# Two-layer hybrid decoder trunk: maxima spread by DRAM transfers, recurrence by pairs, one norm ahead of its transposes, six late value chunks

## Chip, cores and metric

The kernel runs on one core of a Trainium2 chip. The metric is the device time of one execution in microseconds, as the median of the runs. A profile is one execution of its own, with its own time.

## What is computed

256 tokens of width 1024 go through two layers. Layer 0 mixes tokens with an mLSTM of 4 heads, layer 1 with an RG-LRU recurrence of width 768; both add cross-attention over 256 memory tokens. Each mixer is followed by an output projection and a norm, and each of these by PEER (128 x 128 experts, chosen by the top 16 of two key halves) and a second norm. Cut to what the change touches:

```python
# mLSTM, here as one block of 256 tokens instead of chunks
F  = cumsum(log_sigmoid(f))              # 4 heads x 256 tokens
M  = running_max(i - F)                  # the gate maxima
w[s, t] = exp((i - F)[s] - M[t])  for s <= t, else 0
h  = (w * (k q)) v / max(|den|, exp(-(F + M)))
# RG-LRU
r, g = sigmoid(x W_a + b_a), sigmoid(x W_x + b_x)
a  = exp(-8 r softplus(-lam));  u = sqrt(1 - a*a) * g * x
h[t] = a[t] * h[t-1] + u[t];    y = h * gelu(gate)
# after each mixer and each PEER
x  = (x - mean) * rsqrt(var + eps) * g + b
```

## The kernel before, in words

All large products run on TensorE as three float32r passes: every operand is split into a high part (a rounded copy, wH) and a low part (wL = w - wH), and `mm3` (L161) forms H·H + H·L + L·H. Small products (`fp32`, L221) run in full fp32, which the trace shows as two matmuls each. The weights come from DRAM as a single list of chunks of 128 x up to 1024 (`plan`, L1080). SP loads them into five raw buffers (`load`, L116), ScalarE casts wH (L96), VectorE or GpSimd subtracts wL (`pump`, L76; `pool_cols` says how many columns GpSimd takes). A ring of three holds the split chunks (`hl`), and `EXTRA` = 3 more (`eH`, `eL`) stand in the mixer's memory for its output projection. `next` (L132) takes the next chunk, splits up to three ahead, and calls `tick` (L147), which advances one step of each generator given to `beside`. So side work enters the engines' queues one step per chunk. Every engine runs its queue in the written order.

**Layer 0** (`mlstm_layer`, L470). The keys and gates are projected first (7 tiles of `w0kg`). Beside the query projection (8 chunks of `w0qx`, `proj_t`) runs `gates` (L510): log sigmoid, the scans F and M, and `keys` (L547), which copies the keys, scaled, out of PSUM on VectorE. Then the memory projection `mem_kv` (L379, 4 chunks). After it M, which stands in 4 partitions, is spread to all 128: `sel` holds a row of ones per head, and for each head TensorE forms sel·M and adds the causal mask by an identity product (L575 to 578), and ScalarE takes the exponential with a bias per partition (L580, L581). Then come the products of keys and queries, multiplied with these weights on VectorE (L589), the cross-attention scores, and the value projection.

**Layer 1** (`rglru_layer`, L663). After the projections and a convolution, `xattn_scores` queues the softmax; three chunks of the output projection are split ahead into `eH`, `eL`, cast and subtracted on VectorE (L715 to 717). Then for six column tiles the gate products and sigmoids (L720 to 732), then `lru` (L733): decay for all six tiles, `xattn_out` (transposes, copies by ScalarE and VectorE in turn, products, split), one square root over all six tiles (L744), and then, for each pair of tiles, the scan, the gate and the split (L754 to 760). The output projection (`proj_n`, L178) runs its chunks in the order 6, 7, 0, 1, 2, 3, 4, 5; with `tail` = 6 the last six chunks are kept: their products for the first 128 tokens all come first, those for the second half last, and the norm of the first half runs beside the latter (`early`).

**Norm** (`norm`, L250) is a generator, whose steps are called between products. `add` adds the bank to x and `half` takes statistics, `stats` the variance, `center` and `spread` scale on VectorE, `scale_beside` on ScalarE and GpSimd, `turn` transposes into xH and xL. **PEER** (`peer_layer`, L916) runs 128 chunks of u, in whose second half the chosen weights are scattered, then 128 chunks of v (`products`, L1044); the last three are kept (`late`) so that the first half's norm can begin. Layer 0's last norm scales, transposes the first two of eight column tiles, scales the rest and leaves the other transposes to steps beside the next projection; ahead of it stands the memory projection of layer 1 with chunks already split. Layer 1's last norm stores the output in quarters.

## Time and profile before

| | us |
|---|---|
| median of 3 runs (1865.24 to 1870.0) | 1867.91 |
| profiled execution: its own time | 1865.7 |
| its span | 1863.9 |
| TensorE busy | 1821.8 (98%) |
| VectorE busy | 1298.0 (70%) |
| ScalarE busy | 940.3 (50%) |
| GpSimd busy | 428.7 (23%) |
| moved from and to DRAM | 333 MB, 179 GB/s |

Times inside the execution count from the start of the span. A TensorE row shows 128 x 128 weights and the columns that pass; rows of the order of time merge neighbouring instructions of one line (xN) and name in brackets the idle time of the engine before them and what ended it. PE is TensorE, DVE VectorE, ACT ScalarE, POOL GpSimd, SP the queue that issues most transfers.

### The profile page before, as it was taken

Reading aid. Unit: us, or ns where it says so; the run is one execution under the profiler, and the core shown is the slowest. Engines: PE = TensorE matmul, PEld = TensorE weight load, DVE = VectorE, ACT = ScalarE, POOL = GpSimd, SP = SyncE. Lnnn points to the kernel's source line nnn. Section 1 sums busy time; section 2 is a strip of 40 time slices with the busy share of each in tenths; the row PEclk is TensorE's granted clock in tenths of the full one; section 3 lists DMA queues with packets and bytes.
Section 4 is the critical chain, followed back from the end, with each engine's and each line's share of the span. In section 5 each row is a group of like instructions: output and inputs, shape, how many; then the busy total and the mean of one; then the engine's idle time right before and its main releaser. Section 6 shows DMA issues by size and latency. Waiting matters only on the chain.

```text
span 1863.9 us, 33272 instructions
## 1 busy us (share of the span) xinstructions
PE 1821.8 (98%) x12770; PEld 1675.5 (90%) x12770; DVE 1298.0 (70%) x2665; ACT 940.3 (50%) x1604; POOL 428.7 (23%) x326
## 2 busy tenths in 40 slices
PE   8999999999999999999998899999999999999997
PEld 8898999999999888888887699999999988888886
DVE  6474579689998555666556638695999975555556
ACT  5454555455545444555537255554555454555543
POOL 2005772343331000000010258425333300000001
PEclk9999999999999999999999899999999999999999
DMA  7465556655555666667644166666555566666664
GB/s 244 132 178 171 179 177 191 199 174 161 165 163 162 196 195 193 193 215 227 205 169 139 59 193 177 198 192 192 160 161 165 162 179 193 193 193 194 193 194 132
DMA packets 94344, 333.42 MB, mean 179 GB/s; under 512 B 10600, under 2 KB 12904, under 8 KB 93928
## 3 DMA queue, kind: packets, MB, share of 16 engines
q1 hardware_dynamic: 93320, 328.66, 58.3%
q10 hardware_dynamic: 864, 2.62, 0.4%
q8 instruction: 100, 1.64, 0.4%
q14 instruction: 60, 0.49, 0.1%
HBM read 330.19 MB, written 1.05 MB: 178 GB/s over the span
## 4 chain that ended last, share of the span: by engine, by line
PE 72%; issue 15%; POOL 7%; DVE 3%; ACT 1%; DMA 1%; SPq 0%; POOLq 0%; ACTq 0%; DVEq 0%
PE bank L164 23%; PE bank L165 23%; PE bank L163 23%; POOL wL L106 7%; PE bank L222 3%; DVE wL L111 1%; DMA raw<-in_w0kg_dram 1%; ACT wH L96 0%; DMA raw<-in_w0qx_dram 0%; DVE xc L700 0%; PE bank L314 0%; DVE aa L747 0%; DVE x L293 0%; POOL wL L109 0%; DVE x L288 0%
## 5 line engine op out<-in xcount | busy, mean ns | idle before, releaser
L96 ACT CAST wH<-raw 128x1024 fp32r<-128x1024 f32 (+2 forms) x608 | 632.3, 1041 | 791.0 <-PE bank L165 330.2
L111 DVE TENSOR_TENSOR wL<-raw,wH 128x1024 fp32r<-128x1024 f32 (+3 forms) x413 | 468.5, 1137 | 455.7 <-ACT wH L96 455.1
L163 PE MATMUL bank<-xHL,wH 128*128 128x256 f32 x2536 | 717.6, 283 | 5.9 <-ACT wH L96 4.5
L165 PE MATMUL bank<-xHL,wL 128*128 128x256 f32 x2536 | 704.5, 278 | 7.3 <-DVE wL L111 7.3
L164 PE MATMUL bank<-xHL,wH 128*128 128x256 f32 x2536 | 704.5, 278 | 0.2
L165 PEld LDWEIGHTS bank<-xHL,wL 128*128 128x128 f32 x2536 | 479.1, 189 | 9.3 <-DVE wL L111 9.1
L163 PEld LDWEIGHTS bank<-xHL,wH 128*128 128x128 f32 x2536 | 479.1, 189 | 6.6 <-ACT wH L96 4.5
L164 PEld LDWEIGHTS bank<-xHL,wH 128*128 128x128 f32 x2536 | 479.6, 189 | 0.9 <-DVE xHL L219 0.9
L165 PE MATMUL bank<-wH,cL 128*128 128x512 f32 x1024 | 398.4, 389 | 0.0
L164 PE MATMUL bank<-wL,cH 128*128 128x512 f32 x1024 | 398.3, 389 | 0.0
L163 PE MATMUL bank<-wH,cH 128*128 128x512 f32 x1024 | 398.3, 389 | 0.0
L109 POOL TENSOR_TENSOR wL<-raw,wH 128x1024 fp32r<-128x1024 f32 (+1 forms) x121 | 258.1, 2136 | 211.7 <-ACT wH L96 181.1
L165 PEld LDWEIGHTS bank<-wH,cL 128*128 128x128 f32 x1024 | 192.2, 188 | 40.0
L163 PEld LDWEIGHTS bank<-wH,cH 128*128 128x128 f32 x1024 | 192.2, 188 | 39.9
L164 PEld LDWEIGHTS bank<-wL,cH 128*128 128x128 f32 x1024 | 192.2, 188 | 39.8
L106 POOL TENSOR_TENSOR wL<-raw,wH 128x386 fp32r<-128x386 f32 x126 | 129.7, 1029 | 279.9 <-DVE wL L104 279.9
L303 POOL TENSOR_TENSOR x<-x,raw 128x256 f32<-128x256 f32 x7 | 5.3, 760 | 614.4 <-ACT x L300 614.4
L878 DVE TENSOR_TENSOR oh<-iota,i12T 128x1024 f16<-128x1024 f16 x128 | 130.5, 1020 | 0.0
L104 DVE TENSOR_TENSOR wL<-raw,wH 128x640 fp32r<-128x640 f32 x126 | 104.0, 825 | 7.4
L881 DVE TENSOR_TENSOR oh<-oh,gT 128x1024 f16<-128x1024 f16 x128 | 90.1, 704 | 4.4
L1011 PE MATMUL bank<-oh 128*128 128x128 f16 x1024 | 81.1, 220 | 1.1 <-DVE oh L881 1.1
L1011 PEld LDWEIGHTS <-oh 128*128 128x128 f16 x1024 | 58.9, 98 | 6.0 <-DVE oh L881 1.5
(269 smaller groups left out, 1524.1 us busy)
## 6 DMA issues: line engine op xcount, KB each, us to landing
raw<-in_u_dram SPq DMA_DIRECT2D x256, 512.0 KB, 3.7
raw<-in_v_dram SPq DMA_DIRECT2D x256, 512.0 KB, 4.3
raw<-in_w_q_dram SPq DMA_DIRECT2D x32, 512.0 KB, 3.7
raw<-in_w_out_dram SPq DMA_DIRECT2D x16, 512.0 KB, 4.5
raw<-in_w0qx_dram SPq DMA_DIRECT2D x8, 512.0 KB, 4.7
raw<-in_wkv_dram SPq DMA_DIRECT2D x8, 512.0 KB, 4.7
raw<-in_w1x_dram SPq DMA_DIRECT2D x8, 512.0 KB, 4.4
raw<-in_w0v_dram SPq DMA_DIRECT2D x8, 384.0 KB, 3.7
```

The source lines that it names most:

```text
L96: (nc.vector.tensor_copy if self.cast_dve else nc.scalar.copy)(h[:, c], r[:, c])
L104: nc.vector.tensor_sub(l[:, k:], r[:, k:], h[:, k:].bitcast(F32))
L106: nc.gpsimd.tensor_sub(l[:, :k], r[:, :k], h[:, :k].bitcast(F32))
L109: nc.gpsimd.tensor_sub(l[:, :k], r[:, :k], h[:, :k].bitcast(F32))
L111: nc.vector.tensor_sub(l[:, k:], r[:, k:], h[:, k:].bitcast(F32))
L163: mm(out, sH, mH, start=start, stop=False, skip_group_check=True)
L164: mm(out, sH, mL, start=False, stop=False, skip_group_check=True)
L165: mm(out, sL, mH, start=False, stop=stop, skip_group_check=True)
L222: self.nc.tensor.matmul(out, lhsT, rhs, start=start, stop=stop, skip_group_check=True)
L878: nc.vector.tensor_tensor(flat(oh[:, 1:3]), self.iota2.unsqueeze(1).to_broadcast([P, 4, P, 2]), pairs(self.i12T[:, j]), op=ALU.is_equal)
L881: nc.vector.tensor_tensor(flat(oh[:, 0:2]), two.rearrange("p z (q e t) -> p z q e t", q=2, t=2), pairs(self.gT[:, j]), op=ALU.mult)
L1011: nc.tensor.matmul(wp[:, qs], oh[:, 2, q // 2, :, q % 2], oh[:, z, q // 2, :, q % 2], start=z == 0, stop=z == 1, skip_group_check=True)
```

## The change

Layer 0: `sel` and its products go. M is stored to a DRAM tile of 4 x 256 and loaded back twice, each time to all 128 partitions, into `pw`, both on ScalarE's queue, from two new last steps of `gates`; GpSimd adds the mask to the diagonal blocks. The gates are cut into more steps, the keys are scaled by ScalarE, and the last step runs in `mem_kv`. Layer 1: decay, root, scan and gating go by pairs of tiles, the first pair's decay after the second of the six gate products; the transposes of the cross-attention come before the sixth; copies and mixer splits go to VectorE; four chunks instead of three are split ahead, with wL by GpSimd, as for the rest of the output projection, which keeps four chunks instead of six. Layer 0's second norm (`fill`) scales everything, splits two more chunks, and does all transposes before the last memory chunk. Layer 1's PEER keeps six value chunks, three of them in buffers `ends` where the low half of the weights lay, and its norm takes the second half's last 512 columns in two steps and stores in another order. The diff, cut to its core:

```diff
 def proj_n(self, splits, stat, order=range(DT), tail=0, hook=(-1, None)):
-        own, ring = late[:EXTRA], late[EXTRA:]
+        own, ring = late[:tail - HL_BUFS], late[tail - HL_BUFS:]
-    def split_to(self, dH, dL, src):
-        self.nc.scalar.copy(dH, src)
+    def split_to(self, dH, dL, src, cast=None):
+        (cast or self.nc.scalar.copy)(dH, src)
 def norm(self, y, last, early, fill=False):
+        fine = early or last
+        if last:
+            root(0)
+            nc.vector.tensor_scalar(nm, mv[:, 0, 0:1], rs[:, 0:1], -1.0, op0=ALU.mult, op1=ALU.mult)
+            scale_beside(0, 2)
+            scale(0, 2, 2), store(nc.sync, 0, 2, 2)
+            store(nc.sync, 0, 0, 2)
+            yield
+            half(*add(1, 0))
+            yield
+            half(*add(1, 1))
+            yield
+            half(*add(1, 2)), stats(1)
+            center(1, 0, 2), root(1)
+            spread(1, 0, 2), store(nc.scalar, 1, 0, 2)
+            center(1, 2, 2)
+            for q in (2, 3):
+                spread(1, q, 1), store(nc.sync, 1, q, 1)
+            return
...
+        if fill:
+            center(1, 0, 2), root(1), spread(1, 0, 2)
+            scale(0, 2, 2), scale(1, 2, 2)
+            self.release("g", "b")
+            self.pump(self.n_got + 2 + HL_BUFS)
+            yield
+            for q in (0, 2):
+                for tt in range(2):
+                    turn(tt, q, 2)
             return
 def mem_kv(self, chunks=None, hook=None):
         for c in range(4):
+            if hook and c == 3:
+                hook()
 def mlstm_layer(self):
-            sel = w.tile([4, 4, P], F32, name="sel")
+            row = ctx.enter_context(tc.tile_pool(name="row", bufs=1, space=DRAM)).tile([4, T], F32, name="row")
+            pw = w.tile([P, 4, 384], F32, name="pw")
...
                 nc.vector.tensor_scalar(M, M, -1.0, None, op0=ALU.mult)
+                yield
+                nc.scalar.dma_start(row, M)
...
                 nc.vector.tensor_scalar(c8, l6, -8.0, None, op0=ALU.mult)
+                yield
+                every = lambda n, o: bass.AP(tensor=row.tensor, offset=row.offset + o, ap=[[0, P], [T, 4], [1, n]])
+                nc.scalar.dma_start(pw[:, :, 0:T], every(T, 0))
+                nc.scalar.dma_start(pw[:, :, T:384], every(P, P))
+                diag = bass.AP(tensor=pw.tensor, offset=pw.offset, ap=[pw.ap[0], [384, 4], [T, 2], [1, P]])
+                nc.gpsimd.tensor_tensor(diag, diag, maskn.unsqueeze(1).unsqueeze(1).to_broadcast([P, 4, 2, P]),
+                                        op=ALU.add)
             def keys(t0, t1):
-                        nc.vector.tensor_scalar(kT[rows, h, part, :], src[rows], 192.0 ** -0.5, None, op0=ALU.mult)
+                        nc.scalar.activation(kT[rows, h, part, :], src[rows], AF.Copy, scale=192.0 ** -0.5)
             qx = self.proj_t(8, X)
-            self.finish_sides()
...
             self.mem_kv()()
+            self.finish_sides()
...
             for h in range(4):
-                W = self.bank()
-                self.fp32(W[:, 0:T], sel[:, h, :], M, True, False)
-                self.fp32(W[:, 0:P], self.ident, maskn, False, True)
-                self.fp32(W[:, T:384], sel[:, h, :], M[:, P:T], False, False)
-                self.fp32(W[:, T:384], self.ident, maskn, False, True)
-                nc.scalar.activation(pw[:, h, 0:T], W[:, 0:T], AF.Exp, bias=ac[:, 0, h:h + 1])
-                nc.scalar.activation(pw[:, h, T:384], W[:, T:384], AF.Exp, bias=ac[:, 1, h:h + 1])
+                nc.scalar.activation(pw[:, h, 0:T], pw[:, h, 0:T], AF.Exp, bias=ac[:, 0, h:h + 1])
+                nc.scalar.activation(pw[:, h, T:384], pw[:, h, T:384], AF.Exp, bias=ac[:, 1, h:h + 1])
 def rglru_layer(self):
-            self.pump(self.n_got + 2 + EXTRA)
+            self.pump(self.n_got + 2)
+            self.pool_cols = D
+            self.pump(self.n_got + 3 + EXTRA)
+            self.pool_cols = MIX_COLS
+            def decay(b):
+                for i in (2 * b, 2 * b + 1):
+                    nc.gpsimd.tensor_mul(rr[:, 1, i, :], xc[:, i, :], rr[:, 1, i, :])
+                    nc.scalar.activation(aa[:, i, :], rr[:, 0, i, :], AF.Exp, scale=c8[:, i:i + 1])
+                    nc.scalar.activation(th[:, i, :], rr[:, 0, i, :], AF.Tanh, scale=n8[:, i:i + 1])
+                    nc.vector.tensor_mul(rr[:, 0, i, :], aa[:, i, :], aa[:, i, :])
+                    nc.vector.scalar_tensor_tensor(th[:, i, :], rr[:, 0, i, :], 1.0, th[:, i, :],
+                                                   op0=ALU.add, op1=ALU.mult)
+            def root(b):
+                nc.scalar.activation(fl(th, b), fl(th, b), AF.Sqrt, bias=self.tiny)
+            def scan(b):
+                nc.vector.tensor_mul(fl(th, b), fl(th, b), fl(rr[:, 1], b))
+                for i in (2 * b, 2 * b + 1):
+                    nc.vector.tensor_tensor_scan(aa[:, i, :], aa[:, i, :], th[:, i, :], 0.0,
+                                                 op0=ALU.mult, op1=ALU.add)
+            def mixed(b, cast=None):
+                nc.vector.tensor_mul(fl(gt, b), fl(gt, b), fl(aa, b))
+                self.split_to(fl(self.mixH, b), fl(self.mixL, b), fl(gt, b), cast)
             for co in range(6):
+                if co == 5:
+                    self.xattn_turn(w2, dve)
...
+                if co == 1:
+                    decay(0)
+            root(0)
+            self.split_to(*self.xattn_out(0), dve)
+            last = self.xattn_out(1)
+            scan(0)
+            self.split_to(*last, dve)
+            mixed(0, dve)
+            decay(1)
+            decay(2)
+            root(1)
+            root(2)
+            scan(1)
+            mixed(1, dve)
+            self.pool_cols = D
-            self.proj_n((512, 512), (self.mixH, self.mixL), (6, 7, 0, 1, 2, 3, 4, 5), HL_BUFS + EXTRA)
+            self.proj_n((512, 512), (self.mixH, self.mixL), (6, 7, 0, 1, 2, 3, 4, 5), HL_BUFS + 1,
+                        (3, lambda: (scan(2), mixed(2, dve))))
 def peer_layer(self, layer):
+            kept = HL_BUFS + (EXTRA if layer else 0)
...
-                if i + 1 > P - HL_BUFS:
+                if i + 1 > P - kept:
                     continue
...
+            if layer:
+                products(0, 0, 512, late), products(0, 512, 512, late)
+                ln = self.norm([y[0], [y[1][0], y[1][1][:, :256], y[1][1][:, 256:]]], True, False)
+                next(ln), products(1, 0, 512, late)
+                next(ln), products(1, 512, 256, late)
+                next(ln), products(1, 768, 256, late)
+                next(ln, None)
...
+            ln = self.norm(y, False, False, True)
...
-            products(1, 1, late), next(ln)
-            out = self.mem_kv(self.kvw) if layer == 0 else None
+            products(1, 512, 512, late), next(ln), next(ln)
+            out = self.mem_kv(self.kvw, lambda: next(ln, None))
```

## Rows read from the trace of the kernel before

**Rows 1.** The page, part 1: busy time, share, instructions by engine

```profile
PE 1821.8 (98%) x12770; PEld 1675.5 (90%) x12770; DVE 1298.0 (70%) x2665; ACT 940.3 (50%) x1604; POOL 428.7 (23%) x326
```

**Rows 2.** Windows by stage: length, busy time by engine, clock, DMA share, GB/s

```profile
28.10:53.10 25.00, 21.55 (x183) 20.78 (x182) 21.01 (x38) 12.64 (x19) 5.77 (x4) 1.00 0.70 227
...
64.50:73.60 9.10, 9.10 (x35) 5.81 (x35) 0.83 (x3) 4.29 (x10) 0.00 (x0) 0.82 0.16 45
73.60:80.60 7.00, 7.00 (x34) 6.20 (x33) 1.66 (x3) 1.45 (x3) 0.00 (x0) 0.74 0.00 0
...
953.00:966.00 13.00, 10.40 (x72) 9.76 (x71) 10.29 (x16) 7.07 (x11) 0.12 (x1) 0.87 0.87 323
...
1023.40:1047.80 24.40, 18.26 (x66) 13.34 (x66) 14.07 (x25) 8.16 (x11) 0.00 (x0) 0.85 0.00 0
1047.80:1066.90 19.10, 16.08 (x78) 13.40 (x78) 11.23 (x24) 4.62 (x8) 8.26 (x19) 0.85 0.40 120
...
1840.00:1853.40 13.40, 13.40 (x61) 11.01 (x59) 9.03 (x16) 6.19 (x9) 0.00 (x0) 1.00 0.14 43
1853.40:1863.90 10.50, 0.30 (x2) 0.00 (x0) 7.29 (x13) 1.06 (x3) 4.84 (x6) 0.77 0.28 100
```

**Rows 3.** Order of time on TensorE, two waits near 960 and 1023

```profile
960.02 0.39 PE L165 MATMUL bank<-xHL,wL 128*128 128x256 f32 x1 [1.95 <-DVE wL L111]
...
1023.41 6.74 PE L222 MATMUL bank<-pT,vm 128*128 128x256 f32 x16 [5.87 <-ACT pT L66]
```

**Rows 4.** Order of time on VectorE behind the last matmul, first and last

```profile
1853.73 0.69 DVE L267 SCALAR_TENSOR_TENSOR x<-x,bank 128x512 f32<-128x512 f32 x1 [0.31 <-PE bank L165]
...
1860.72 0.48 DVE L293 SCALAR_TENSOR_TENSOR x<-x,rs,raw 128x256 f32<-128x256 f32 x1
```

**Rows 5.** Windows of two stretches at the lower clock

```profile
70.40:77.30 6.90, 6.90 (x20) 5.23 (x20) 0.56 (x1) 2.19 (x5) 0.00 (x0) 0.51 0.00 0
...
1046.60:1053.40 6.80, 6.28 (x14) 4.58 (x15) 4.79 (x5) 1.78 (x2) 0.00 (x0) 0.50 0.65 205
```

**Rows 6.** Order of time, VectorE and GpSimd beside the query projection, 35 to 41

```profile
35.21 0.41 DVE L527 SCALAR_TENSOR_TENSOR gt<-gt 4x256 f32<-4x256 f32 x1
35.55 1.50 DVE L528 SCALAR_TENSOR_TENSOR gt<-g,gt 4x256 f32<-4x256 f32 x1
...
38.45 1.28 DVE L551 TENSOR_SCALAR kT<-bank 64x256 f32<-64x256 f32 x3
39.65 1.22 DVE L111 TENSOR_TENSOR wL<-raw,wH 128x1024 fp32r<-128x1024 f32 x1
...
35.48 1.30 POOL L109 TENSOR_TENSOR memL<-raw,memH 128x512 fp32r<-128x512 f32 x1 [4.43 <-ACT memH L96]
```

**Rows 7.** Groups by line on ScalarE, 64.5 to 84

```profile
L580 ACT ACTIVATE pw<-bank,ac 128x256 f32<-128x256 f32 x4 | 1.9, 474 | 5.0 <-PE bank L222 5.0
```

**Rows 8.** Transfers by name: count, KB each, us to landing

```profile
raw<-in_ln_g_dram SPq DMA_DIRECT2D x4, 512.0 KB, 4.8
...
wb<-in_rg_blk_dram ACTq DMA_DIRECT2D x1, 1792.0 KB, 8.4
...
out_dram<-x ACTq DMA_DIRECT2D x2, 128.0 KB, 1.8
```

**Rows 9.** Groups by line on GpSimd, 1000 to 1066

```profile
L109 POOL TENSOR_TENSOR wL<-raw,wH 128x1024 fp32r<-128x1024 f32 x2 | 4.7, 2386 | 0.0
```

**Rows 10.** Groups by line on VectorE, 1009 to 1052: scan, square

```profile
L747 DVE TENSOR_TENSOR_SCAN aa<-aa,th 128x256 f32<-128x256 f32 x6 | 4.1, 692 | 0.2
...
L738 DVE TENSOR_TENSOR rr<-aa 128x256 f32<-128x256 f32 x6 | 2.5, 421 | 6.4 <-ACT th L737 6.4
```

**Rows 11.** Order of time on VectorE: the last pair's subtraction

```profile
1045.57 0.69 DVE L219 TENSOR_TENSOR mixL<-gt,mixH 128x512 fp32r<-128x512 f32 x1 [0.68 <-ACT mixH L218]
```

**Rows 12.** Groups by line on ScalarE, 1000 to 1047: a table load

```profile
L736 ACT ACTIVATE aa<-rr,c 128x256 f32<-128x256 f32 x6 | 3.0, 496 | 0.0
...
L736 ACT ACT_TABLE_LOAD x1 | 1.3, 1283 | 0.0
```

More of the change, by code (lines that the diff above doesn't have):

```diff
@@ L16 @@
 PSUM = bass.MemoryType.PSUM
+DRAM = bass.MemoryType.DRAM
 P = 128
@@ L247, in constants, with norm @@
         tmp.__exit__(None, None, None)
-    def norm(self, y, last, early):
+    def norm(self, y, last, early, fill=False):
         nc, x = self.nc, self.x
+        fine = early or last
         while "b" not in self.kept:
@@ L261, in add @@
         def add(tt, k):
-            if early and tt and k:
+            if fine and tt and k:
                 q0, n = 1 + k, 1
@@ L270, in half @@
         def half(tt, q0, n):
-            if early and tt:
+            if fine and tt:
                 for q in range(q0, q0 + n):
@@ L277, in stats @@
         def stats(tt):
-            n = 4 if early and tt else 2
+            n = 4 if fine and tt else 2
             nc.vector.bn_aggr(mv[:, tt, :], st[:, tt, :n].rearrange("p a b -> p (a b)"))
@@ L337, in norm @@
         half(*part)
-        if not last:
-            self.pool_cols = D
-            self.pump(self.n_got + 2 + (2 if early else 1))
-            self.pool_cols = MIX_COLS
+        self.pool_cols = D
+        self.pump(self.n_got + 2 + (2 if early else 1))
+        self.pool_cols = MIX_COLS
         if early:
@@ L349, in norm @@
         stats(1)
-        if last:
-            scale(0, 3, 1), store(nc.sync, 0, 3, 1)
-            root(1)
-            scale(1, 0, 2), store(nc.scalar, 1, 0, 2)
-            for q in (2, 3):
-                scale(1, q, 1), store(nc.scalar, 1, q, 1)
+        if fill:
[7 more added lines that the diff above has]
+                    turn(tt, q, 2)
             return
@@ L436, in xattn_scores, with xattn_turn @@
         self.beside(softmax())
-    def xattn_out(self, w):
+    def xattn_turn(self, w, copy):
         nc = self.nc
-        def turn(h):
+        self.pts = []
+        for h in range(4):
             p = self.bank()
@@ L596, in mlstm_layer @@
             self.finish_sides()
-            self.xattn_out(w)
+            self.xattn_turn(w, self.copy)
+            for hp in range(2):
+                self.split_to(*self.xattn_out(hp))
             nb = []
@@ L1114, in tail @@
             for i in range(P):
-                self.add(A["v"][layer, i], D)
+                e = i - P + HL_BUFS + EXTRA
+                self.add(A["v"][layer, i], D, e if layer and 0 <= e < EXTRA else None)
                 k = (i - N0 - 4) // 6
```

124 lines of the change are left out of this document (51 added, 73 removed).

## Prediction

> **What bounds the kernel now.** I read the page's busy times first, then busy time and granted clock by stage, then TensorE's own waits, and last the order of time on VectorE, ScalarE and GpSimd around each wait. TensorE is busy 98% of the span [rows 1], so 42 us is all its idle time. The windows [rows 2] show where it lies: 3.45 us between 28.1 and 53.1, 2.6 between 953 and 966, 6.1 between 1023.4 and 1047.8, 3.0 up to 1066.9, and 10.2 after the last matmul; TensorE's own rows add 5.87 just before 1023.4 [rows 3], and behind the last add VectorE alone needs 7.5 us [rows 4]. At the lower of the clock's two levels (1.2 instead of 2.4 GHz) TensorE runs in two stretches of 6.9 and 6.8 us [rows 5], and for about 3.4 us of 953 to 966 (0.87 granted over 13.0), which costs 1.7. The long PEER loops in between have almost no idle to give back, and the change leaves them as they are. So its worth is idle time, low clock and removed matmuls, at five places. The gap tiles, the earlier close of the right-hand pool and the renamed buffers move no work and count nothing.
>
> **1. Keys and gates beside the query projection.** TensorE waits here for wL from VectorE, which stands at gate arithmetic and key scaling: three keys cost 1.28 us just ahead of the late wL at 39.65 [rows 6], and there are eight. The change gives the keys to ScalarE and spreads the rest over more steps. VectorE loses 8 x 0.42 = 3.4 us. ScalarE gains as much or a little more (0.47 for 256 columns from PSUM [rows 7]), and behind its keys queue its own casts of wH, which pace wL. I take 1.0 us of stall as left: **gain 2.4**, bounds 0 and 3.4.
>
> **2. Gate maxima.** Sixteen fp32 products go, that is the 9.1 us window from 64.5 [rows 2] but for 0.3 us of transposes: 8.8. Of the low stretch from 70.4 to 77.3 [rows 5] 3.7 us lie in the score products behind them; ahead of it ran products with four rows, which are gone, so I give back half of 3.7: **gain 10.6**, bounds 7.0 and 10.6. New are one store of 4 KB and two loads of 768 KB on ScalarE's queue, and one GpSimd add of 1024 columns. The store is nearest the 128 KB store at 1.8 us; the loads lie between the 512 KB broadcast at 4.8 and 1.75 MB at 8.4 [rows 8]; the add is nearest 2.39 [rows 9]. The loads go out near 51, in the first step of the memory projection, beside SP's loads of norm weights, x and value chunks, wanted only later. ScalarE waits for the store there, with the memory chunks' casts behind it, but a whole chunk lies between store and loads, so it has landed. 51 + 8.4 + 2.4 = 61.8. The eight exponentials (at most 8 x 0.47 [rows 7]) begin near 64, behind copies and a table load, and must begin by 67: their banks are wanted after 5.2 us of scores and 3.3 of cross-attention. So I price the round trip at 0; with that cover gone each us late costs one.
>
> **3. Norm between the layers.** The four transposes now stand ahead of the last quarter of the memory projection, and all scaling and two more chunk splits ahead of them. The 2.6 us of idle, 1.95 of it at wL [rows 3], goes, and with it I expect the low stretch right behind: **gain 4.3**, bounds 1.5 and 4.3.
>
> **4. Recurrence by pairs.** Idle of 5.87 and 6.1 and half of 13.7 us at the low clock make 18.8 at most. What is late next is VectorE. From the first pair's root on it does three pairs of multiply 0.69, two scans of 0.69, multiply 0.69, cast 0.4 and subtract 0.69 [rows 10, 11], 3.9 us each; the decay of two pairs, 8 x 0.42; and two cross-attention splits, 1.6: 16.7 together. I put that root's end at 1021.6: softmax ends at 1009.8, then four table loads (one more than the old order) at 1.3, 12 sigmoids and 4 exponentials at about 0.38 start to start and a 0.6 us root. Two more loads come later, beside VectorE's chain. A load takes 1.28 and the activation behind it shows no idle [rows 12]. The Trainium skill (ScalarE: Activation LUTs, What ACT_TABLE_LOAD costs) puts a switch at about 2.66 us with its drain; by that the three new ones would cost 4.1 more, a gain here of 6 instead of 10. No run here shows that drain.
> Then collisions. GpSimd now makes wL of four chunks early and of two at the end, 2.39 us each [rows 9], while VectorE works on pairs of SBUF operands. A 4-row VectorE operation that takes 0.41 took 1.50 beside one GpSimd subtraction of 1.30 [rows 6]. I charge 3.2: 1021.6 + 16.7 + 3.2 = 1041.5 for the last pair, against 1046.3 [rows 11]. After it TensorE has 8.7 us left, not some 17: four chunks kept instead of six (two at 2.66), the rest clock and late wL. The early norm loses cover, so its 3.0 us of idle [rows 2] grows by 2.2. The query projection then starts near 1057 instead of 1067: **gain 10**, bounds 7 and 13.2 (no collision).
>
> **5. Six value chunks for the end.** The last products now hide the first half's norm for 8 us instead of 4. The chunk split last waits for a slot that comes free as the long stretch begins: cast and subtraction of 1.22 each [rows 6] and its coefficients make 2.9, and it is wanted after 15 products of 0.22 (13.4 us for 61 [rows 2]), 3.3. If that is missed, each us late costs one. Behind the last matmul VectorE needs add 0.41, statistics 0.43 and 0.26, centre 0.75, root 0.15, scale 0.75, centre 0.75, 2 x 0.48: 4.5 us, against 7.5 from 1853.73 to 1861.2 [rows 4]. **Gain 3.0**, bounds 1.5 and 3.5.
>
> **Sum.** 2.4 + 10.6 + 4.3 + 10 + 3.0 = 30.3. The profiled execution took 1865.7 us (span 1863.9), 2.2 below the median of 1867.9. 1865.7 - 30.3 = 1835.4; against the median **1837.5**. The low bounds sum to 17 (1851), the high ones to 35.0 (1833).
>
> **Rivals.**
> The lock in full: VectorE and GpSimd hand each other SBUF for whole instructions, as the 1.50 us operation [rows 6] suggests. Two subtractions of 2.39 on the last chain and one ahead of the first root then cost 7 instead of 3.2, and part 3 loses 1 to another: 1842. For: the stretched row. Against: much of GpSimd's work ends before VectorE's chain begins. The Trainium skill (SBUF — State Buffer, Who interferes with whom) states this rule: an exclusive lock on a shared port pair, between a VectorE instruction with two SBUF inputs and a GpSimd one that reads SBUF. The rows agree with it.
> No collisions: part 4 gives 13.2, 1834.3. For: the early subtractions can run beside the softmax. Against: the same row.
> The low clock stays: in these rows it falls behind waits and behind products of little work. If it falls behind the smaller new waits too, 6.8 in part 4, 1.8 in part 2 and 1.7 in part 3 come back, and part 1 gives nothing: 1850. Against: none is seen behind the waits of part 1.
> Slower: the round trip of pw. Place: ScalarE's wait for the stored maxima, then GpSimd's add ahead of the exponentials, with the value chunks' casts behind. It costs from 67 on and makes the kernel slower than before only past 67 + 30 = 97, 46 us after the issue; the slowest load in the rows takes 8.4 [rows 8]. At 110 the time is 1881.
> It doesn't do what it says: each wait only moves one place on (wL behind ScalarE's keys, the last pair no earlier, the stores as late), and the value projection waits out what part 2 frees: near 1867.
>
> **How the numbers follow.** Forecast 0.50, lock in full 0.20, no collisions 0.12, low clock stays 0.11, moved waits 0.04, slower 0.03. The range 1829 to 1851 takes in the first four and the bounds, with 4 us below the high ones for the two small wL waits of the conv stage. About 0.3% (5.6 us) is what a measurement of this kernel can tell from no change; all of the first four lie past it: faster 0.93, within it 0.04, slower 0.03.
>
> **What would show it.** Right: no products with four rows, scores directly behind the memory projection at full clock; no wait on wL near 958; no wait of 5.9 for pT, but waits of one to two us for mixH and six table loads in the recurrence; VectorE operations of 1.5 to 2.9 us beside GpSimd's wL; 7 to 8 us between the last matmul and the end. Wrong: a value projection that waits for its banks, ScalarE idle at pw, PEER chunks that come at another pace, low clock through the scores.

## The result, and the profile after

The changed kernel takes 1843.11 us (median of 4 runs, 1842.5 to 1843.62) against 1866.95 of the kernel before on the same chip (median of 4, 1865.24 to 1870.0, the three of the table ahead and one more): a ratio of 0.9871, 95% interval 0.9855 to 0.9886, so 23.8 us or 1.3% faster. The profiled executions took 1865.7 and 1843.52 us (spans 1863.9 and 1841.7), 22.2 apart. Forecast were 30.3 and 1837.5; the gain fell 6.5 short and the time came out 5.6 above, as the fourth run had moved the median of before down by 1.0.

Where the 22.2 us lie is read from TensorE's order of time: the start of the first product of each stage, in both traces.

| Part | stage (from, to) | before | after | gained | forecast |
|---|---|---|---|---|---|
| 1 | start to first memory product | 53.16 | 52.46 | 0.70 | 2.4 |
| 2 | to the start of the value projection | 30.74 | 20.13 | 10.61 | 10.6 |
| 2 | value projection | 16.83 | 17.31 | -0.48 | 0 |
| | layer 0's first norm: first transposes to first sub-key product | 34.09 | 35.07 | -0.98 | 0 |
| 3 | layer 1's memory projection to its cross-attention scores | 58.83 | 53.27 | 5.56 | 4.3 |
| 4 | scores to first output product | 29.71 | 26.13 | 3.58 | |
| 4 | to the first transposes of the norm | 30.89 | 28.38 | 2.51 | 10 in all |
| 4 | to the first sub-key product | 33.87 | 34.85 | -0.98 | |
| 5 | layer 1's value chunks to the last matmul | 348.34 | 349.52 | -1.18 | |
| 5 | behind the last matmul | 10.22 | 7.31 | 2.91 | 3.0 in all |

The stages left out differ by 0.08 together. With the value projection counted in, part 2 came out 0.5 under its forecast; part 3 came out 1.3 over it. Part 4 gave 5.1 of 10, part 1 fell 1.7 short and part 5 1.3, and a norm that nobody had touched lost 1.0.

The page, part 1, after, against [rows 1]: 14 fewer TensorE instructions, 13.3 us less busy, 22.2 us less span. VectorE and GpSimd are busier, by 9.3 and 17.4 us.

```profile
PE 1808.5 (98%) x12756; PEld 1667.9 (91%) x12756; DVE 1307.3 (71%) x2653; ACT 940.9 (51%) x1606; POOL 446.1 (24%) x330
```

Windows by stage of the kernel after (the columns of [rows 2]). In order: part 1's query projection; gate transposes and scores; cross-attention scores; value projection; end of layer 1's memory projection; transposes to first output product in the recurrence; output projection up to a wait, and on to the norm; the norm's wait; the last value chunks; behind the last matmul.

```profile
27.46:52.46 25.00, 23.56 (x200) 22.95 (x198) 16.55 (x22) 15.88 (x28) 6.49 (x4) 1.00 0.72 237
63.72:69.33 5.61, 5.61 (x36) 5.13 (x36) 0.83 (x3) 2.07 (x4) 1.57 (x1) 1.00 0.54 201
69.33:72.59 3.26, 3.26 (x18) 2.87 (x17) 1.33 (x3) 2.44 (x7) 0.79 (x1) 1.00 0.00 0
72.59:89.90 17.31, 17.18 (x98) 16.68 (x97) 13.13 (x25) 11.17 (x28) 0.00 (x0) 1.00 0.43 132
939.90:944.50 4.60, 4.60 (x43) 4.60 (x42) 4.57 (x7) 2.55 (x5) 0.00 (x0) 1.00 0.92 293
1002.50:1010.90 8.40, 8.36 (x40) 7.63 (x40) 7.10 (x14) 4.51 (x10) 2.92 (x4) 0.80 0.13 48
1010.90:1025.79 14.89, 11.46 (x62) 9.73 (x60) 14.48 (x22) 9.04 (x14) 5.13 (x2) 1.00 0.12 35
1025.79:1039.28 13.49, 12.58 (x55) 9.48 (x55) 9.19 (x17) 2.58 (x4) 1.53 (x3) 0.87 0.14 40
1039.28:1045.93 6.65, 2.06 (x12) 1.45 (x12) 4.75 (x13) 1.45 (x4) 6.65 (x17) 0.86 0.43 103
1820.00:1834.44 14.44, 13.93 (x77) 11.78 (x75) 7.34 (x15) 1.18 (x3) 3.28 (x4) 1.00 0.10 36
1834.44:1841.70 7.26, 0.00 (x1) 0.00 (x0) 4.23 (x9) 0.29 (x1) 0.00 (x0) 0.84 0.20 72
```

Three readings. The four-row products are gone and the scores run at 1.00 where they had 0.74. The end of the memory projection, with all four groups of transposes in it, has no idle. In the recurrence VectorE is busy 14.48 of the 14.89 us in which TensorE idles 3.4.

The order of time of the kernel after shows the waits. First TensorE, five of its waits (left out are 4.38 us ahead of the very first product and 2.65 in layer 0's norm):

```profile
41.19 0.39 PE L166 MATMUL bank<-xHL,wL 128*128 128x256 f32 x1 [1.02 <-DVE wL L112]
...
1002.54 0.33 PE L465 MATMUL bank<-ident,pr 128*128 128x128 f32 x1 [3.68 <-DVE pr L453]
...
1025.79 0.50 PE L164 MATMUL bank<-eH,mixH 128*128 128x512 f32 x1 [3.43 <-DVE mixH L219]
...
1044.79 0.47 PE L316 MATMUL bank<-ident,x 128*128 128x128 f32 x1 [4.13 <-DVE x L295]
...
1832.05 0.38 PE L164 MATMUL bank<-eH,cH 128*128 128x256 f32 x1 [0.51 <-DVE x L269]
```

The 5.87 us wait for pT [rows 3] became 3.68 for the scaled softmax, and the wait for the second pair's mixH is 3.43 where one to two were forecast. Now what VectorE, GpSimd and ScalarE did ahead of these two (a merged row xN gives the sum; the ScalarE row is the first pair's root):

```profile
989.23 4.05 DVE L97 CAST eH<-raw 128x1024 fp32r<-128x1024 f32 x3
993.20 2.84 DVE L97 CAST wH<-raw 128x1024 fp32r<-128x1024 f32 x1
...
996.19 8.03 DVE L453 TENSOR_SCALAR pr<-pr,sm 128x256 f32<-128x256 f32 x8
...
990.00 8.25 POOL L110 TENSOR_TENSOR eL<-raw,eH 128x1024 fp32r<-128x1024 f32 x3 [45.20 <-DVE eH L97]
998.21 2.40 POOL L110 TENSOR_TENSOR wL<-raw,wH 128x1024 fp32r<-128x1024 f32 x1
...
1009.98 0.72 ACT L762 ACTIVATE th<-th,tiny 128x512 f32<-128x512 f32 x1
...
1020.50 2.76 DVE L771 TENSOR_TENSOR gt<-gt,aa 128x512 f32<-128x512 f32 x1
1023.29 2.45 DVE L219 CAST mixH<-gt 128x512 fp32r<-128x512 f32 x1
...
1029.13 0.43 DVE L219 CAST mixH<-gt 128x512 fp32r<-128x512 f32 x1
1029.60 0.69 DVE L220 TENSOR_TENSOR mixL<-gt,mixH 128x512 fp32r<-128x512 f32 x1
...
1020.32 5.13 POOL L110 TENSOR_TENSOR wL<-raw,wH 128x1024 fp32r<-128x1024 f32 x2 [10.85 <-ACT wH L97]
```

The same cast of 512 columns takes 0.43 with GpSimd still (1029.13) and 2.45 beside its subtraction; the multiply of 0.69 takes 2.76. The first root ends 25.9 us behind the scores of its stage (984.77); the prediction had it at 21.5 (1021.6 with the scores at 1000.09). The last pair's subtraction starts at 1029.60, which is 44.8 us behind these scores; before it was 45.5 [rows 11, with the scores at 1000.09]. The chain that part 4 was to shorten ended almost where it had.

Behind the last matmul VectorE has 4.4 us left instead of 7.5 [rows 4]:

```profile
1834.48 0.42 DVE L269 SCALAR_TENSOR_TENSOR x<-x,bank 128x256 f32<-128x256 f32 x1 [2.02 <-PE bank L166]
...
1838.00 0.88 DVE L295 SCALAR_TENSOR_TENSOR x<-x,rs,raw 128x256 f32<-128x256 f32 x2
```

### The profile page after: what moved, and what is told of

It reads as the page before. It is cut to its first block, busy times and chain, and to the rows that moved or that the text cites. A ratio compares the mean times of both kernels' runs of the same rounds, so it can differ in the third digit from the quotient of the medians.

```text
span 1841.7 us, 33231 instructions
## 1 busy us (share of the span) xinstructions
PE 1808.5 (98%) x12756; PEld 1667.9 (91%) x12756; DVE 1307.3 (71%) x2653; ACT 940.9 (51%) x1606; POOL 446.1 (24%) x330
## 4 chain that ended last, share of the span: by engine, by line
PE 70%; issue 17%; POOL 8%; DVE 2%; ACT 2%; DMA 1%; SPq 0%; POOLq 0%; DVEq 0%; ACTq 0%
PE bank L166 23%; PE bank L164 23%; PE bank L165 23%; POOL wL L107 7%; PE bank L223 2%; DVE wL L112 0%; DMA raw<-in_w0kg_dram 0%; POOL wL L110 0%; ACT wH L97 0%; ACT pr L447 0%; PE bank L316 0%; DVE xc L727 0%; DMA raw<-in_w0qx_dram 0%; DMA raw<-in_xT_dram 0%; DMA cp<-in_rg_par_dram 0%
## 5 line engine op out<-in xcount | busy, mean ns | idle before, releaser
L112 DVE TENSOR_TENSOR wL<-raw,wH 128x1024 fp32r<-128x1024 f32 (+3 forms) x407 | 460.5, 1134 | 448.5 <-ACT wH L97 446.2
L165 PE MATMUL bank<-wL,cH 128*128 128x512 f32 x1015 | 394.3, 388 | 0.0
L166 PE MATMUL bank<-wH,cL 128*128 128x512 f32 x1015 | 394.3, 388 | 0.0
L164 PE MATMUL bank<-wH,cH 128*128 128x512 f32 x1015 | 394.3, 388 | 0.0
L110 POOL TENSOR_TENSOR wL<-raw,wH 128x1024 fp32r<-128x1024 f32 (+1 forms) x124 | 266.5, 2152 | 223.5 <-ACT wH L97 222.7
```

Source lines behind the costliest of these rows:

```text
L110: nc.gpsimd.tensor_sub(l[:, :k], r[:, :k], h[:, :k].bitcast(F32))
L112: nc.vector.tensor_sub(l[:, k:], r[:, k:], h[:, k:].bitcast(F32))
L164: mm(out, sH, mH, start=start, stop=False, skip_group_check=True)
L165: mm(out, sH, mL, start=False, stop=False, skip_group_check=True)
L166: mm(out, sL, mH, start=False, stop=stop, skip_group_check=True)
```

## Experiments

Theory at the start: GpSimd's subtractions hold up VectorE far more than the 3.2 us charged, and that is most of the shortfall. Rival: VectorE's own work sets the chain, and the stretched rows would have waited for something anyway. The smaller losses got a theory each. All times below are medians beside the kernel before on the same chip; the changed kernel stands at 1843.1. The kernel before stood at 1866.95 beside it and at 1864.95 to 1866.71 beside the runs below, so a difference of 2 us between totals of two chips says little. These are the stage lengths read as above, which tell more than the totals:

| run | first memory product | value projection | layer 0's norm | layer 1 memory to scores | scores to output product | to transposes | to sub-keys | last value chunks | median us |
|---|---|---|---|---|---|---|---|---|---|
| before | 53.16 | 16.83 | 34.09 | 58.83 | 29.71 | 30.89 | 33.87 | 348.34 | 1866.95 |
| after | 52.46 | 17.31 | 35.07 | 53.27 | 26.13 | 28.38 | 34.85 | 349.52 | 1843.11 |
| e1 | 50.64 | 17.46 | 33.93 | 53.26 | 27.33 | 27.24 | 34.30 | 349.52 | 1840.6 |
| e2 | 53.38 | 16.83 | 34.08 | 53.27 | 21.07 | 28.10 | 34.32 | 349.54 | 1836.9 |
| e3 | 52.17 | 16.82 | 33.96 | 53.24 | 26.41 | 28.28 | 34.17 | 349.56 | 1841.73 |
| e4 | 52.27 | 17.95 | 33.93 | 53.24 | 27.32 | 28.31 | 35.30 | 349.56 | 1844.42 |
| e5 | 49.39 | 16.83 | 34.08 | 53.26 | 25.90 | 28.31 | 34.65 | 349.53 | 1839.73 |
| e6 | 53.18 | 16.83 | 35.16 | 53.27 | 26.12 | 28.37 | 34.89 | 348.77 | 1841.12 |
| e7 | 50.61 | 16.84 | 33.99 | 53.26 | 26.12 | 28.29 | 35.40 | 349.52 | 1852.58 |
| e8 | 51.18 | 17.28 | 34.02 | 58.65 | 26.15 | 28.52 | 34.91 | 349.53 | 1846.57 |
| e9 | 49.25 | 16.83 | 35.10 | 53.26 | 21.07 | 28.32 | 34.31 | 348.75 | 1833.72 |
| e10 | 49.18 | 16.83 | 34.04 | 53.26 | 21.07 | 27.10 | 34.25 | 348.74 | 1831.12 |
| e11 | 49.33 | 16.83 | 35.06 | 53.47 | 26.12 | 28.39 | 34.94 | 349.56 | 1840.36 |
| e12 | 51.45 | 18.23 | 33.99 | 53.46 | 27.33 | 28.76 | 35.10 | 349.52 | 1843.12 |

**e1: the last two wL on VectorE.**

```diff
             mixed(1, dve)
-            self.pool_cols = D
             self.proj_n((512, 512), (self.mixH, self.mixL), (6, 7, 0, 1, 2, 3, 4, 5), HL_BUFS + 1,
```

> The changed kernel with the last two wL of layer 1's output projection subtracted by VectorE instead of GpSimd. Theory (lock): beside these two GpSimd subtractions (2.39 and 2.79) a 0.69 multiply took 2.76 and a 0.43 cast 2.45, 4.1 us on the chain to the last pair; on VectorE one subtraction of 1.22 stands ahead of the last scan and one behind it. So the last pair's subtraction starts about 2.9 earlier, the early norm with it, TensorE's wait of 3.43 for mixH falls under 1.5, and the time is near 1840.2, 2.9 under the changed kernel's 1843.1 (1.5 to 3.5). Rival (VectorE's own work sets the chain, the stretched rows would have waited for something anyway): 1.2 to 2.4 more work on VectorE, time 1843 to 1845.5.

1840.6 us (0.9867, 0.9852 to 0.9882). VectorE, order of time in this run:

```profile
1018.80 0.69 DVE L771 TENSOR_TENSOR gt<-gt,aa 128x512 f32<-128x512 f32 x1
1019.52 0.43 DVE L219 CAST mixH<-gt 128x512 fp32r<-128x512 f32 x1
...
1020.60 1.22 DVE L112 TENSOR_TENSOR wL<-raw,wH 128x1024 fp32r<-128x1024 f32 x1
...
1024.95 0.69 DVE L220 TENSOR_TENSOR mixL<-gt,mixH 128x512 fp32r<-128x512 f32 x1
```

The multiply and the cast are back at 0.69 and 0.43, and from the second pair's first multiply (1016.77 here, 1018.47 after) to the last pair's subtraction it takes 8.18 instead of 11.13: 2.95, as expected. TensorE's wait for mixH is 2.33, not under 1.5. The table shows why the profile gains less: 1.1 from the output product to the transposes and 0.5 behind them, but 1.2 lost ahead of the output product, where the low stretch (TensorE at the lower clock level) beside the wait for pr is 6.8 instead of 3.4 us long. So the total of 2.5 is not this chain's alone, the run began 1.8 earlier too. The run shows the lock on the chain; it doesn't price it.

**e2: all six wL of this stage on VectorE** (with e1's edit).

```diff
-            self.pool_cols = D
             self.pump(self.n_got + 3 + EXTRA)
-            self.pool_cols = MIX_COLS
```

> As the run before, and the four early wL of layer 1's output projection on VectorE too. Theory (lock): two casts of 2.85 and 2.84 go back to 0.69 and the softmax scalings of 2.21, 2.44 and 0.81 to 0.35, for four subtractions of 1.22; the scaling ends near 998.8 instead of 1004.2, TensorE's wait of 3.68 for pr goes, the first root starts about 3.7 earlier, and with the 2.9 of the run before the time is near 1836.5 (1834.5 to 1839). Rival (no blocking, only VectorE's work counts): 4 x 1.22 more ahead of the softmax scaling, the wait for pr grows to some 8 us, time 1845 to 1849.

1836.9 us (0.9867, interval 0.9829 to 0.9905; one execution of six at 1859.6 lifts the ratio and widens the interval, the other five lie between 1836.3 and 1837.2, and the medians alone give 0.9845). VectorE, ScalarE's first root, and TensorE, order of time:

```profile
994.21 0.69 DVE L97 CAST wH<-raw 128x1024 fp32r<-128x1024 f32 x1
994.93 1.23 DVE L112 TENSOR_TENSOR wL<-raw,wH 128x1024 fp32r<-128x1024 f32 x1
...
996.31 2.97 DVE L453 TENSOR_SCALAR pr<-pr,sm 128x256 f32<-128x256 f32 x8
...
1005.43 0.72 ACT L760 ACTIVATE th<-th,tiny 128x512 f32<-128x512 f32 x1
...
1022.09 0.69 DVE L220 TENSOR_TENSOR mixL<-gt,mixH 128x512 fp32r<-128x512 f32 x1
...
1022.20 0.47 PE L164 MATMUL bank<-wH,mixH 128*128 128x512 f32 x1 [2.43 <-DVE mixH L219]
```

Though VectorE now makes 7.3 us of subtractions itself, the scaling ends at 999.3 instead of 1004.2, eight scalings take 2.97 instead of 8.03, and the wait for pr falls from 3.68 to 0.30. From the scores (984.17 here) to the first output product 5.06 us are gained; the first root ends 22.0 behind the scores instead of 25.9, and the last pair's subtraction ends 38.6 behind them instead of 45.5. The rival, 1845 or more, is out.

**e3: TensorE kept at work in the norms' waits.**

```diff
...
+        j = self.bank()
+        for _ in range(17 if self.layer else 10):
+            nc.tensor.matmul(j, self.mixH[:, 0, :P], self.extra[0][0][:, :512], start=True, stop=True,
+                             skip_group_check=True)
         center(1, 0, 1)
...
```

> The changed kernel with products that nobody reads (10 in layer 0, 17 in layer 1, 128x512, 0.227 each) put into TensorE's waits of 2.65 and 4.13 us for the normed second half in the norms between output projection and PEER. Theory (the clock falls because of these waits): the low stretches of 6.8 us behind both waits go, 3.4 us are gained at each, time near 1836.5 (1836 to 1840). Rival (the clock falls for something else that stays, such as the short transposes): no change of the low stretches, time 1843 to 1843.7.

1841.73 us (0.987, 0.9855 to 0.9885). Half of the theory holds, the half that counts falls. The changed kernel runs at the lower level (1.2 GHz) behind both waits; its windows:

```profile
142.90:149.70 6.80, 6.34 (x29) 5.83 (x29) 5.91 (x9) 1.81 (x3) 2.20 (x8) 0.50 0.25 86
1044.00:1050.80 6.80, 5.55 (x23) 4.99 (x24) 5.47 (x10) 1.42 (x2) 3.53 (x16) 0.50 0.42 123
```

With the waits filled both stretches are at 1.00 throughout, but TensorE then stands at the next operand (e3, a window and TensorE's order of time):

```profile
1040.00:1056.00 16.00, 13.93 (x103) 12.48 (x102) 12.91 (x20) 5.51 (x8) 8.58 (x20) 1.00 0.62 185
```

```profile
1052.20 0.39 PE L166 MATMUL bank<-xHL,wH 128*128 128x256 f32 x1 [1.21 <-DVE xHL L221]
```

By the table, layer 0's norm takes 33.9 to 34.1 in the eight profiles with a low stretch of 3.4 us there, and 33.96 and 34.04 in the two with none; only the long one of 6.8 (after, e6, e9, e11) costs, 1.1. So 1.1 and 0.7 were gained where 3.4 twice was expected, and even the 0.7 isn't the clock's alone, since e1, e2 and e9 take 34.3 to the sub-keys of layer 1 with the long stretch there. The low clock there lies beside VectorE's scaling and splitting, which sets the pace.

**e4: the round trip of pw one step later.**

```diff
                 yield
+                yield
                 every = lambda n, o: bass.AP(tensor=row.tensor, offset=row.offset + o, ap=[[0, P], [T, 4], [1, n]])
```

> The changed kernel with the two loads of the spread gate maxima issued one memory chunk later (2.83 us). Theory: pw now comes 0.5 us before the value projection wants its fourth bank (the multiply of head 3 ends at 73.6, its first product there stands at 74.15), so the round trip is hidden with 0.5 us to spare, and a shift of 2.8 gives waits of about 2.3 us in the value projection and 2.3 us more in the time. Rival (the cover is several us, since banks come free in another order): no wait, the value projection starts where it did, time unchanged.

One time, 1844.42 us. The shift came out much smaller than meant: the loads went out at 55.33 instead of 54.35 and pw landed at 68.07 instead of 67.61. The value projection took 17.95 instead of 17.31, neither 2.3 more nor unchanged, and the changed kernel run again took 18.23 (e12), so this run alone settles nothing. The changed kernel, order of time on GpSimd, ScalarE and VectorE, and its transfers from 50 to 72:

```profile
67.76 2.36 POOL L575 TENSOR_TENSOR pw<-pw,maskn 128x1024 f32<-128x1024 f32 x1 [22.54 <-DMA pw<-row]
...
70.16 0.51 ACT L605 ACTIVATE pw<-pw,ac 128x256 f32<-128x256 f32 x1 [4.31 <-POOL pw L575]
...
71.68 1.94 DVE L614 TENSOR_TENSOR pw<-pw,bank 128x384 f32<-128x384 f32 x3
```

```profile
x<-in_x_dram SPq DMA_DIRECT2D x1, 1024.0 KB, 8.4
...
pw<-row ACTq DMA_DIRECT2D x1, 256.0 KB, 12.8
```

What settles it are all twelve profiles with the round trip, if the end of VectorE's last multiply with pw (73.62 above) is set against the first product of the value projection (72.59). Where it came at most 0.25 us behind that product (e2, e3, e5, e6, e9, e10, e11), the projection took 16.83; where it came 0.99, 1.02, 1.18, 1.66 and 1.97 behind (e8, the changed kernel, e1, e4, e12), it took 17.28, 17.31, 17.46, 17.95 and 18.23. So about half a us was covered, and each us past that went with one us more. The waits that these profiles name there are for wL of the value chunks (two of 0.2 us in e12), not for a bank.

**e5 and e11: what paces part 1.** e5 loads the recurrence's parameters early and scales five keys later; e11 does the load alone.

```diff
+            nc.sync.dma_start(self.cp, A["rg_par"])
             kg = self.proj_t(7, X)
-            nc.sync.dma_start(self.cp, A["rg_par"])
...
```

> The changed kernel with the load of the recurrence's parameters (cp) issued ahead of the first projection, and with five of the eight keys scaled two or three steps later, when ScalarE is free. Theory (ScalarE now paces part 1): it stands 2.5 us at an exponential whose input waits for cp, and five keys stand ahead of the two casts of wH behind which TensorE waits 0.42 and 1.02; both waits fall under 0.3, and the time is about 1.2 lower, near 1842. Rival (loads and VectorE pace it): waits of the same sum elsewhere before the memory projection, time 1842.5 to 1843.6. The start of the memory projection alone doesn't tell, it lay between 50.6 and 53.4 in five runs with the same work ahead of it.

> The changed kernel with only the load of cp issued ahead of the first projection; the keys stay where the change has them. In the run with both, the memory projection began at 49.4 instead of 50.6 to 53.4 in eight others. Theory (ScalarE's stand at the exponential that needs cp is the cause): start near 49.5, time near 1839.7. Rival (the five keys ahead of the casts are the cause): ScalarE's wait of 2.5 is gone, TensorE's wait of 1.0 behind the keys stays, start 50.6 to 53.4, time 1841 to 1843.

1839.73 us (0.9862, 0.9847 to 0.9877) and 1840.36 (0.9864, 0.9847 to 0.988). The load alone does it: memory projection at 49.33, with both at 49.39, while the changed kernel and the eight runs that left this part alone lay between 50.61 and 53.38. ScalarE and VectorE in the kernel after, then ScalarE in e11:

```profile
33.52 0.17 DVE L535 SCALAR_TENSOR_TENSOR s<-cp 128x6 f32<-128x6 f32 x1 [2.79 <-DMA cp<-in_rg_par_dram]
...
33.73 0.21 ACT L539 ACTIVATE s<-s 128x6 f32<-128x6 f32 x1 [2.50 <-DVE s L535]
```

```profile
30.69 0.19 ACT L539 ACTIVATE s<-s 128x6 f32<-128x6 f32 x1
...
31.56 1.05 ACT L97 CAST wH<-raw 128x1024 fp32r<-128x1024 f32 x1
```

A 6-column exponential for layer 1 stands in ScalarE's queue ahead of the next cast of wH, and waits 2.5 us for a load issued only behind the first projection. With the load early that cast starts 3.1 us sooner, and TensorE's waits for wL up to the memory projection fall from 2.4 us to one of 0.6. TensorE's whole idle time up to there falls from 6.7 to 5.2 us, half of the 3.1 by which the memory projection comes earlier; the other half is products that follow each other faster, for a reason that wasn't found. The kernel before had the same wait, 1.70:

```profile
31.92 0.21 ACT L520 ACTIVATE s<-s 128x6 f32<-128x6 f32 x1 [1.70 <-DVE s L516]
```

The keys, which the prediction blamed and e5's expectation too, cost nothing that these runs can tell.

**e6: the last pieces in another order.**

```diff
...
-                next(ln), products(1, 0, 512, late)
-                next(ln), products(1, 512, 256, late)
-                next(ln), products(1, 768, 256, late)
+                next(ln), products(1, 0, 256, late)
+                next(ln), products(1, 512, 512, late)
+                next(ln), products(1, 256, 256, late)
```

> The changed kernel with the last three column pieces of the value phase in another order: 256 columns of the first bank, 512 of the second, the other 256 of the first, so that TensorE never writes a bank that VectorE is just adding from. Theory (the wait of 0.51 for x behind the piece of 256 is that shared bank): the wait goes, the last matmul ends 0.5 earlier, VectorE's work behind it stays, time near 1842.6. Rival (the end is set by the norm of the first half or by the stores): the wait goes and the end stays, 1843.1, or VectorE is late with the piece of 512 and the end moves back by up to 0.3.

1841.12 us (0.9867, 0.9852 to 0.9882). The wait of 0.51 is gone and the value chunks take 348.77 instead of 349.52, with 7.31 behind the last matmul as before the edit: 0.75 by the stage. It is more than the idle the row names, since the product behind that wait came 0.79 after the one before it instead of 0.12. Of the 1.18 lost there 0.43 remains; nearly half of it is that 36 products of 256 columns follow each other at 0.1185 where 18 of 512 took 0.2267 each. The Trainium skill (PSUM — Partial Sum Buffer, PSUM bank collisions raise a hardware error) says to guard PSUM between engines by bank, not by address; here that is a wait between two halves of one bank that share no number.

**e7: part 2 undone,** the maxima spread by sixteen products again.

```diff
...
-                nc.scalar.activation(pw[:, h, 0:T], pw[:, h, 0:T], AF.Exp, bias=ac[:, 0, h:h + 1])
+                W = self.bank()
+                self.fp32(W[:, 0:T], sel[:, h, :], M, True, False)
...
+                nc.scalar.activation(pw[:, h, 0:T], W[:, 0:T], AF.Exp, bias=ac[:, 0, h:h + 1])
```

> The changed kernel with the gate maxima spread by sixteen fp32 products again, as before, all else as changed. Theory: part 2 is worth the 8.8 us of these products and 1.7 of low clock in the scores behind them, less 0.5 that the round trip now costs in the value projection: time near 1853.2 (1851.5 to 1854). Rival (the low stretch had another cause and falls elsewhere, or other waits take the place): 1850 (the low bound of 7) or less, with no low stretch behind the products.

1852.58 us (0.9927, 0.9913 to 0.994), 9.5 above the changed kernel, though it began 1.85 earlier. Its windows, from the memory projection to the products of keys and queries, and the low stretch:

```profile
50.61:72.37 21.76, 21.76 (x132) 17.75 (x131) 8.16 (x16) 9.87 (x17) 0.00 (x0) 0.85 0.50 186
65.90:76.10 10.20, 10.20 (x28) 7.24 (x28) 0.56 (x1) 2.91 (x7) 0.00 (x0) 0.50 0.00 0
```

The low stretch returned with the products, 10.2 us long, and began while they ran. Up to the value projection the run took 32.1 us where the changed kernel takes 20.1. Both halves of part 2's sum stand.

**e8: part 3 undone.**

```diff
-            ln = self.norm(y, False, False, True)
+            ln = self.norm(y, False, False)
...
-            out = self.mem_kv(self.kvw, lambda: next(ln, None))
+            out = self.mem_kv(self.kvw)
             right.close()
+            next(ln, None)
```

> The changed kernel with the norm between the layers as before (transposes behind the memory projection, scaling behind them), all else as changed. Theory: idle of 2.6 us and a low stretch of 3.4 us behind it come back, and the early splits go: 5.6 by the stages, time near 1848.5. Rival (the low clock near 961 came by chance): only the idle comes back, 1845.5 to 1846.

1846.57 us (0.99, 0.9885 to 0.9915), 3.5 above the changed kernel; the stage took 58.65 again, 5.4 more. The spans differ by 3.1, because this run began 1.3 earlier and had the short norm in layer 0 (1.0). TensorE's order of time, and the window behind it:

```profile
947.48 0.39 PE L166 MATMUL bank<-xHL,wL 128*128 128x256 f32 x1 [2.03 <-DVE wL L112]
```

```profile
948.20:951.60 3.40, 3.40 (x19) 3.40 (x18) 2.16 (x4) 0.00 (x0) 0.00 (x0) 0.51 0.99 365
```

Wait and low stretch return together, at the same place in the work, so the low clock near 961 was no chance. The total alone, nearer to the rival's 1846 than to 1848.5, would not have told.

**e9 and e10: the remedies joined.** e9 has e2, e5 and e6 in one kernel, e10 the filling products too (8 more ahead of the last pair).

> All six wL of layer 1's output projection on VectorE, the early load of cp and the later keys, and the other order of the last pieces, in one kernel. If the three causes are separate, their measured gains add: 6.2 for the wL, 0.7 for the last pieces by TensorE's stage, and between 1.2 and 3.4 for part 1, so 1833 to 1835. If they share one cause (say, all of them only shift where the low clock falls), the sum falls short: 1836 or more.

> As the joined kernel, with products that nobody reads (128x512) in TensorE's wait for the last pair (8 of them) and in the waits of both norms between output projection and PEER (10 and 17). Theory (a wait of 2 us and more there brings the low clock): no low stretch between 100 and 1500; behind the last pair 1.2 us are gained, behind the norms at most 0.5, since there the wait for xHL takes the place of the low clock as in the filler run; 1831 to 1833.5. Rival (the low clock behind the last pair is covered as well): the same time as the joined kernel.

1833.72 us (0.9827, 0.9814 to 0.984) and 1831.12 (0.9814, 0.9801 to 0.9828), 9.4 and 12.0 under the changed kernel, and better than both kernels. By the stages the gains add (5.06 ahead of the first output product, 0.77 in the last value chunks, 3.2 at the start), so the causes are separate; totals from different chips are too coarse for that sum. TensorE ahead of the last pair, e9 and then e10:

```profile
1019.01 0.47 PE L164 MATMUL bank<-wH,mixH 128*128 128x512 f32 x1 [2.43 <-DVE mixH L219]
```

```profile
1017.87 0.47 PE L165 MATMUL bank<-wH,mixH 128*128 128x512 f32 x1 [0.63 <-DVE mixH L228]
```

In e10 no low stretch is left up to the last matmul. Behind the last pair that is worth 1.22, as expected; layer 0's norm gains 1.06 and not at most 0.5, because e9 had the long stretch there.

**e12: the changed kernel again.**

> The changed kernel itself once more, beside the kernel before on the same chip. If the start of the memory projection differs by chance between runs (50.6 to 53.4 so far), the time lies between 1840.5 and 1843.6 and the start differs from 52.46; every other stage keeps its length to 0.1, but for 0.5 in the value projection and 1.1 in the stretch behind each of the two norms.

1843.12 us (1841.45 to 1845.43; 0.9876, 0.986 to 0.9893). The start moved (51.45), but the expectation was too tight: the value projection took 18.23, the stage ahead of the output product 27.33, a low stretch of 6.8 us as in e1 and e4. A profile of one execution fixes these stages to about 1.4 us, no better.

## Why the prediction was right in sign and 5.6 us too low

The time lies inside the range, but nearer to the rival "lock in full" (1842, chance 0.20) than to the forecast, and part 4 below shows that this rival is what happened. That it came no further off is in part luck: part 3 gave 1.3 more than forecast, by a pace of products that nobody had counted.

**Part 1, wrong in size and cause.** 0.70 instead of 2.4 in the profile; -0.2 to 2.5 if the nine starts are set against this one profile of before. "Behind its keys queue its own casts" named the right queue and the wrong instruction: ScalarE stood at an exponential that waits for a load. The step that failed is that VectorE's late wL was put down to VectorE's work without following ScalarE's row ahead of it. e11 shows the cause: without that wait the memory projection begins 3.8 earlier than in the profile of before, 1.2 to 4.2 earlier than in the nine (four starts against nine). The kernel before has the wait too, so this isn't what the change alone is worth.

**Part 2, right.** 10.61 to the value projection, 10.6 forecast: 8.8 by the products, 1.7 by the low clock behind them, for which half of the 3.7 us stretch was forecast, and 0.1 in the memory projection. The round trip, priced at 0, cost 0.48 here and between 0 and 1.4 in other runs (e4). That "with that cover gone each us late costs one" held; the banks as the place of the wait did not. The loads went out at 54.35, not 51, and took until 67.61: I had estimated at most 8.4 us from a transfer without much company, and these ran, the smaller behind the larger, beside x, norm weights and value chunks. The exponentials began 3 us past the limit of 67, and cost so little because they take 2.9 us instead of 3.8 and hand their banks over head by head. That the crowded transfers are the cause is argued from the rows; other queues were not tried.

**Part 3, right, under-sized.** 5.56 instead of 4.3. Idle fell from 4.2 to 1.7 us, and the low stretch went, as forecast, 1.7; e8 shows both. The rest, 1.3, was in no row I had read: without idle and low clock the products behind the memory projection took 0.119 us each in the kernel before and in e8, and 0.115 now. Why is open.

**Part 4, the step that failed.** "I charge 3.2" for collisions: the term was mis-sized, and it cost 7.3. Counted from the scores, the forecast has the last pair's split end at 41.4 us (1041.5 with the scores at 1000.09), 38.2 without collisions; it ended at 45.5 in the changed kernel and at 38.6 in e2. Of the 7.3, 4.4 lie ahead of the first root, where the early subtractions were taken to cost next to nothing. Against the free durations the rows show casts 4.0 us longer (6.8 from 989.23 to 996.04 instead of four of 0.69), scalings 5.1 longer, multiply and cast on the last chain 4.1 longer: 13 us, not all of it on the chain. I had counted only VectorE operations with two SBUF inputs, and taken the early subtractions as hidden by the softmax. With GpSimd out of the way (e2) the three stages give 10.98 between 13.2, the upper bound, and the 10 of the forecast; so the rest of the working, the load of VectorE's chain among it, holds, but for one sum: 4.8 for the earlier last pair and 8.3 behind it, less 2.2, make 10.9 and not 10. The rival "lock in full" was the case that happened; it priced the collisions at 7. The Trainium skill (SBUF — State Buffer, Who interferes with whom) states also the half that I left out: copy, cast and a scaling by a scalar can take both port pairs and are then locked out by GpSimd as well. These rows agree with it, 0.69 to 2.84 for a cast. I had weighed another rule of the Trainium skill, a table switch of 2.66 us with its drain (ScalarE: Activation LUTs, What ACT_TABLE_LOAD costs), by which part 4 would give 6 by my estimate: e2's 10.98 with the same loads speaks against it here, and in the changed kernel the next activation starts 0.01 us behind six of the seven loads from the scores on, and 0.36 behind the last.

**Part 5, half right.** The tail gained 2.91, as forecast; 1.18 was lost ahead of the last matmul, 0.75 of it to the shared bank, which the prediction did not look for: the second half's last 512 columns in two steps were read as VectorE's affair, not as a conflict with TensorE's next write. No run took part 4's pairs or part 5 back as a whole, so 5.1 and 2.91 are read from the stages alone.

**Clock.** The last rival (1850) took the low stretches behind new waits as costs in full. They came behind waits of 2.3 us (e1) and more, though not behind each one (none behind 3.42 in e4), and e3 shows that behind the norms they are mostly covered. The 0.98 lost in layer 0's norm is a long stretch in place of a short one, which four of the thirteen profiles but that of before show; in layer 1 the stretch behind the norm's wait was long in every one that did not fill it.

## What to carry to other kernels

Before work moves to GpSimd, list every VectorE instruction that would run beside it, casts and scalings from SBUF included, and charge each the whole GpSimd instruction; 1.22 us on VectorE was far cheaper here than 2.39 on GpSimd. When an engine is late, read its queue backwards to the first instruction that waits for something outside; a small operation meant for later may stand there for a load. A low clock had its full price here only where the next step waited for TensorE.

## What the runs showed that was not expected

- With the same work ahead of it, the memory projection began anywhere between 50.6 and 53.4; with one small load issued earlier it began between 49.2 and 49.4 in four runs.
- The 768 KB of pw, read back from DRAM to all partitions in two loads, landed 9.5 to 13.2 us after the issue of the second load in twelve profiles (12.8 in the changed kernel), while 1 MB of x beside them took 8.4.
- In the same place of the work the low stretch is 3.4 us long in some runs and 6.8 in others, and products of 256 columns follow each other at 0.113 or 0.118 at full clock; what decides either wasn't found.
